# A two-layer encoder trunk on one core: latents scaled on ScalarE, key and value units inside gates, a mask column for the last heads' sums, output projection by half sums

## The chip, the core and the metric

The kernel runs on one core of a Trainium2 chip. The metric is the device time of one execution in microseconds. TensorE (PE, with its weight loads PEld), VectorE (DVE), ScalarE (ACT), GpSimd (POOL) and SyncE (SP, which issues most DMAs) each work through a queue of their own in order and meet at semaphores.

## The reference, cut to what matters

512 tokens of width 1024 pass two layers. Each layer is, in fp32:

```python
h = rms_norm(x, attn_norm_g[l])
proj = h @ w_in[l]
c_q, c_kv, k_rope, gq, gk, gv, pool_in, gate_logits = split_columns(proj, IN_SIZES)
o_mla = mla_branch(c_q, c_kv, k_rope, ...)   # q = rms_norm(c_q) @ w_uq, k and v = rms_norm(c_kv) @ w_ukv
o_gqa = gqa_branch(gq, gk, gv, ...)
o_pool = pool_branch(pool_in, ...)
merged = (gates[:, :, 0] * (o_mla @ w_branch_mla[l])
          + gates[:, :, 1] * (o_gqa @ w_branch_gqa[l])
          + gates[:, :, 2] * (o_pool @ w_branch_pool[l]))
x = x + merged @ w_out[l]
hf = rms_norm(x, ffn_norm_g[l])
u = depthwise_conv(hf @ ffn_w_up[l], ffn_conv_w[l], ffn_conv_b[l])
x = x + (silu(u_gate) * u_val) @ ffn_w_down[l]
```

The latents are c_q (256 columns) and c_kv (128); each is divided by its own root mean square before it meets its weights. Both attentions have eight heads.

## The kernel before

**Numbers in two parts.** Every matmul operand is kept as a large part (hi) and the rest (lo), and a product is three matmuls (mm3, line 378): hi with hi, hi with lo, lo with hi. Activations lie as features by tokens, 512 tokens in the free dimension, in the tiles HH and HL.

**The weights' stream.** All weights lie in HBM as one stream of pieces of up to 512 columns, in the order of use (_widths and _stream, lines 83 to 100; _pack_weights, line 1609). SP loads slots of up to 1024 columns into three buffers (raw, w_dma). w_split (line 326) makes the parts of a piece: ACT copies hi (tile wh), POOL or VectorE subtracts lo (tile wl). wnext (line 363) keeps three pieces ahead.

**An order written by a planner.** The instructions are issued by hand, in an order that a small clock in the program decides (class Clock, line 126): it books an estimated cost on each engine, chains of steps are put in when their estimated time has come, and a question like ck.has(key) asks whether a result should be there. The result is a fixed order on every engine; on the chip semaphores make each instruction wait for what it really needs.

**A layer.**
- tok_major (line 579) computes the latents, tokens by columns, for four blocks of 128 tokens, into four PSUM banks.
- norm_begin and norm_finish (lines 466 and 474) make the RMS norm's factor: VectorE transposes and reduces the sum of squares (tile prt), a matmul of 16 columns adds it over partitions (ps_S<-prt,C), POOL takes the power, VectorE spreads the result (rt by token, rbc by column). norm_finish is tried after each step of the pool matmuls that follow the latents, and carried out once the clock says that prt is there, or by force at one step.
- latents (line 640): ACT empties the four banks (lat_evac) and sums squares, POOL takes the power (ssc), lat_norm scales the four blocks in tile mx on VectorE, eight instructions. lat_turn (line 701) transposes each block on VectorE, writes it to DRAM, reads it back in twelve DMAs as features by tokens, and splits it on ACT (cth) and VectorE (ctl).
- The pool branch's matmuls (line 692), the queries of the second attention (tok_major into gqb, line 747) with their squares, sums and rotations (gq_square, gq_rope), then its keys and values, with the pool's product between (pool_product, line 789). The rotations free the queries' banks.
- gates (line 871) yields the three branches' matmuls in units: a gate tile (eight units of three matmuls), a branch tile (four), and between them the units of the first attention's queries, keys and values (make_q, make_n, make_v; keys and values are 256 columns wide and share two PSUM banks, acc, with the gates). _order (line 66) lists them from EXTRA; a generator of units (Filler, line 103) is spent beside the attention's matmuls to keep TensorE busy.
- attention (line 1131): a plan of times places each head's steps. o_out (line 1306) puts a pair of heads' results and sums into order; the row of the sums that is no result is set to 0 by POOL, then it is added.
- The output projection (line 1438): eight output tiles, one after the other, each over eight merged tiles (kc), which the last branch delivers one by one: product, sum (XM), hi on ACT (mgh), lo on VectorE (mgl).
- The feed-forward part, which is the longest, and then the next layer.

Of the kernel before, what the change touches and what calls it, by code (L numbers as in the profile page):

```python
# [18 lines left out]
P = 128  # L19
# [11 lines left out]
WIDE = 528  # L31
NWIDE = 5
RAW = 3
EXTRA = (("q", 2, (2, 5)), ("n", 2, (6, 7)), ("v", 1, (2, 5)))

SOONER = {1: 3 * KC, 0: 6 * KC}
LAG = {2: 1, 1: 4, 0: 8}
# [2 lines left out]
PRE_B = 8  # L40
LA = 3
END = object()
RSQRT_BITS = 1597463007.0
SLACK = 35
PLAN = {"gqa": (-4.2, -1.0, -0.2, 0.0, 0.65, 2.411, 4.57, 32.003),
        "mla": (-6.2, -2.9, -1.0, 0.1, 0.64, 1.678, 1.82, 35.5)}

D_ROW, D_OUT, D_IN, D_LAT = 3.4, 3.2, 4.0, 6.0
D_FREE = 0.8
REST = 0.4  # L50
W_BIAS = 2.54
C_BIAS = 0.2
# [11 lines left out]


def _order(br):


    r, lag = [], LAG[br]
    for m in range(KC + lag):  # L70
        r += [(k, pos.index(m)) for k, b, pos in EXTRA if b == br and m in pos]
        if m < KC:
            r.append(("g", m))
        if m >= lag:
            r.append(("b", m - lag))
    return r
# [6 lines left out]
def _widths():  # L83

    r = [384] * KC + [T] * 8 + [T] * KC + [288] * 4 + [T] + [288] * 4
    for br in (2, 1, 0):
        for k, _ in _order(br):
            r += WIDTHS[k]
    return r + [T] * (2 * KC) + [T] * (4 * FC) + [T] * (2 * FC)


# [34 lines left out]
class Clock:  # L126
# [37 lines left out]
    def done(self, *key):  # L164
        self.ready[key] = self.fin + self.SEM
# [90 lines left out]
def trunk(ctx: ExitStack, tc: tile.TileContext, x, w, prm, gb, cst, out):  # L256
# [134 lines left out]
    ident = C[:, C_ID:C_ID + P]  # L391
    mhalf = cp.tile([P, 1], F32, tag="mhalf", name="mhalf")
    eps = cp.tile([P, 1], F32, tag="eps", name="eps")


    MQ, MK = [[cp.tile([P, 4, 4, 96], F32, tag=f"{n}{g}", name=f"{n}{g}") for g in range(2)] for n in ("MQ", "MK")]
# [76 lines left out]

    def norm_finish(gen, out, force=False):

        if gen not in parts or not (force or ck.has(("prt", gen))):
            return
        need(("prt", gen))
        s2 = ps("S")
        mm(s2[:, :16], C[:, C_GRP:C_GRP + P], parts.pop(gen), True, True)  # L480
        a, a4 = small("fac", [P, 16]), small("fac4", [P, 16])
        rt, rbc = out["rt"], out["rbc"] = small("rt", [P, 4]), slot("rbc")

        def mean():
            V.tensor_scalar(a, s2[:, :16], 1.0 / D, EPS, ALU.mult, ALU.add)
            free("S")

        def tokens():
            V.tensor_tensor(a4, a, C[:, C_SEL:C_SEL + 16], ALU.mult)
            V.tensor_reduce(rt, a4.rearrange("p (b g) -> p b g", g=4), AX.X, ALU.add)  # L490
            done("rt", gen)

        def rows():
            V.transpose(rbc[:, :T].rearrange("p (j r) -> p j r", r=32), bc(a.unsqueeze(2), [P, 16, 32]))
            done("rbc", gen)

        chain(mean, lambda: G.tensor_tensor(a, a, bc(mhalf, [P, 16]), ALU.pow), tokens, rows, after=0.3)
# [43 lines left out]
    def layer(l, sq, xsrc):  # L541
# [89 lines left out]
            for c0, n in ((0, 256), (1, 128)):  # L631
                V.tensor_scalar(ssc[:, :, c0:c0 + 1], ssc[:, :, c0:c0 + 1], 1.0 / n, EPS, ALU.mult, ALU.add)

        def lat_norm():
            for b in range(4):
                V.tensor_scalar(mx[b][:, 0:256], mx[b][:, 0:256], ssc[:, b, 0:1], None, ALU.mult)
                V.tensor_scalar(mx[b][:, 256:384], mx[b][:, 256:384], ssc[:, b, 1:2], None, ALU.mult)
            done("lat", l)

        def latents():  # L640
            chain(*[([("rt", G1)], lambda b=b: lat_evac(b)) for b in range(4)], lat_mean,
                  *rsqrt_steps(ssc.rearrange("p a b -> p (a b)"), 8, ("ssc", l)), lat_norm)

        latents()

# [46 lines left out]
        for g in range(4):  # L692
            acc = ps(ptags[g])
            for n, _ in enumerate(feat_major(acc, G1)):
                norm_finish(G1, nrm, g == 1 and n == 6)
            chain(*pool_steps(g, acc, ptags[g]))


# [2 lines left out]
        def lat_turn():  # L701
            d = dp.tile([4, P, 384], F32, tag=f"dl{l}", name=f"dl{l}")
            trs, tos = [], []

            def turn_block(b):
                trs.append(slot("tr"))
                V.transpose(trs[b][:, :384], mx[b][:, :384])

            def put(b):
                SY.dma_start(d[b], trs[b][:, :384])  # L710
                ck.fin = ck.now + (D_OUT if b == 3 else 0.1)

            def get(j):
                to = slot("tf")
                src = d.rearrange("b (i f) (c t) -> c f (b i) t", i=4, t=32)
                for c in range(4):
                    SY.dma_start(to[32 * c:32 * c + 32, :T].rearrange("f (g t) -> f g t", t=32), src[4 * j + c])
                chain(*split(lat[j][0][:, :T], lat[j][1][:, :T], to[:, :T], col(PRM_CQ + j)),
                      lambda: done("latT", l, j), after=D_LAT)
                ck.fin = ck.now + 1.5  # L720

            steps = []
            for b in range(4):
                steps += [lambda b=b: turn_block(b), lambda b=b: put(b)]
            chain(*steps, *[lambda j=j: get(j) for j in (2, 0, 1)], after=0.1)

        chain(([("lat", l)], lat_turn))


        qtags = ("AV", "AV", "mi", "ST")  # L730
# [19 lines left out]
        def gq_square(b):  # L750
            j = slot("gqs")
            A.activation(j[:, :T], gqb[b], AF.Square, scale=rtok(b))

            def sums():
                V.tensor_reduce(ssr[:, 8 * b:8 * b + 8], j[:, :T].rearrange("p (h f) -> p h f", f=64),
                                AX.X, ALU.add)
                done("gqs", l, b)

            chain(sums, after=ck.fin - ck.now + 0.1)

        def gq_rope(b):
            q, o = (t.rearrange("p (h f) -> p h f", f=64) for t in (gqb[b], gqo[b][:, :T]))
            cs = bc(tabs[0][:, None, 64 * b:64 * b + 64], [P, 8, 64])
            sn = bc(tabs[0][:, None, 256 + 64 * b:320 + 64 * b], [P, 8, 64])
            parts, add = rope_steps(o, q, cs, sn, [P, 8, 64], 32, V, G)
            parts()
            free(qtags[b])
            chain(add, lambda: done("gqr", l, b), after=ck.fin - ck.now)

        def gq_mean():  # L770
# [100 lines left out]
        def gates(br, okey, odst, mode):  # L871
# [44 lines left out]
                    merged[m] = (mh, ml)  # L916
                    chain(product, add, *split(mh[:, :T], ml[:, :T], XM[:, m, :]), fin)

            extra, tick, gap = None, 0, 2
            for k, m in _order(br):  # L920
                if k in mla_make:
                    extra, tick, gap = mla_make[k](m), 0, 2 if k == "q" else 4
                    continue
                work = branch(m) if k == "b" else gate(m)
                more = True
                while more:
                    if extra and tick % gap == 0:
                        if next(extra, END) is END:
                            extra = None
                        yield  # L930
                    tick += 1
                    more = next(work, END) is not END
                    yield
# [197 lines left out]
        def attention(kind, fill, okey, odst):  # L1131
# [174 lines left out]
            def o_out(h):  # L1306
# [16 lines left out]

                def add():

                    for j in (0, 64):
                        G.memset(sums[j:j + 1, :T], 0.0)
                    (V if h == 7 else G).tensor_tensor(raw[:, :T], raw[:, :T], sums[:, :T], ALU.add)

                steps = [copies]  # L1330
                if h % 2 == 1:
# [103 lines left out]

        sq = slot("sq")
        tags = ("acc", "ST", "AV", "mi", "S")
        for m in range(KC):
            tag = tags[m % 3]
            acc = ps(tag)  # L1440
            for kc in range(KC):
                if kc % 4 == 0:
                    wh, wl = wnext()
                need(("mrg", l, kc))
                ws = slice((kc % 4) * P, (kc % 4) * P + P)
                mm3(acc, wh[:, ws], wl[:, ws], merged[kc][0][:, :T], merged[kc][1][:, :T], kc == 0, kc == KC - 1)

            def resid(m=m, acc=acc, tag=tag):
                V.scalar_tensor_tensor(XM[:, m, :], acc, 0.5, XM[:, m, :], ALU.mult, ALU.add)
                free(tag)  # L1450

            chain(resid, *norm_steps(G2, m, col(PRM_FG + m), sq))
# [105 lines left out]
    A.activation(warm, warm, AF.Exp)  # L1558
    V.memset(mhalf, -0.5)
    V.memset(eps, EPS)  # L1560
    G.memset(f(unit), 0.0)
    G.memset(f(unit[:, 0:1]), 1.0)
    idle = ps("mi")
# [45 lines left out]
def _pack_weights(i):  # L1609
    res = []  # L1610
    for l in range(L):
# [13 lines left out]
        uq, ukv = i["mla_w_uq"][l], i["mla_w_ukv"][l].reshape(P, 8, P)  # L1625

        wb = (i["w_branch_mla"][l], i["w_branch_gqa"][l], i["w_branch_pool"][l])
        for br in (2, 1, 0):
            for k, m in _order(br):
                c = slice(m * P, m * P + P)  # L1630
                if k == "g":
                    res += _cut(_blocks(gate[:, br * D:(br + 1) * D][:, c], KC))
                elif k == "b":
                    res += _cut(_blocks(wb[br][:, c], 4))
                elif k == "q":
                    res += [uq[kc * P:kc * P + P, m * 384:m * 384 + 384] for kc in range(2)]
                else:
                    c = slice(0, 64) if k == "n" else slice(64, P)
                    res.append(ukv[:, 4 * m:4 * m + 4, c].reshape(P, 256))
        for m in range(KC):  # L1640
            res += _cut(_blocks(i["w_out"][l][:, m * P:m * P + P], KC))
        up = i["ffn_w_up"][l]
        for c in range(FC):
            for o in (0, D_FF):
# [85 lines left out]
```

## Time and profile before

| what | value |
|---|---|
| median of three runs | 1575.72 us (1575.36 to 1576.02) |
| the profiled execution's own time | 1576.64 us |
| its span, first to last instruction | 1574.2 us |
| TensorE busy | 1564.2 us, 99% |
| POOL, VectorE, ACT busy | 1021.7, 955.3, 787.4 us |
| granted TensorE clock | 1.00 |
| mean DMA rate | 104 GB/s |

The span is one execution, and the time around it (2.4 us) belongs to start and end. In a row of the timeline stand the start, the duration, the engine, the line of the program (a helper's, so that most rows are told apart by their tiles: what is written, an arrow, what is read), the shape, the count, and in brackets the idle time before it with what ended it. A row with a count merges neighbours of one kind, with the time from the first one's start to the last one's end. In the table of waits stand the time in all, the number of times and the longest.

### The profile page before, as it was taken

The page shows a single profiled execution, that of the slowest core. Times are in us where ns is not written, and L with a number is a line of the kernel's source. Part 1 is how long each engine was busy: PE and PEld are TensorE (multiplying, and loading weights), DVE is VectorE, ACT ScalarE, POOL GpSimd, SP SyncE. Part 2 cuts the span into 40 slices and gives each one's busy share as a digit, 9 for nine tenths or more (in the row PEclk, how much of TensorE's full clock was granted, in tenths as well). Part 3 has the DMA queues.
Part 4 walks back from the last instruction along what each step waited for, and adds up shares of the span by engine and source line. Part 5 has one row for each costly group of instructions (what it writes and reads, how often), then busy time and mean ns, then how long its engine had stood idle before and what let it go on. Part 6 is the DMA issues. An engine that isn't in the chain of part 4 may idle for free.

```text
span 1574.2 us, 20365 instructions
## 1 busy us (share of the span) xinstructions
PE 1564.2 (99%) x7098; PEld 1308.7 (83%) x7098; DVE 955.3 (61%) x1360; ACT 787.4 (50%) x1426; POOL 1021.7 (65%) x890
## 2 busy tenths in 40 slices
PE   9999999999999999999999999999999999999999
PEld 8888888888888888888898888888888888888888
DVE  6877967866267767720047788678652777777000
ACT  5357866763444444432244677676534444444221
POOL 3874987854667666654578649868547766666542
PEclk9999999999999999999999999999999999999999
DMA  5432234314333332333335322343252223233331
GB/s 200 124 113 76 76 95 138 114 56 139 113 95 94 94 105 86 105 107 110 117 103 136 104 75 75 115 136 96 70 158 93 90 95 98 94 96 105 108 128 47
DMA packets 85926, 164.43 MB, mean 104 GB/s; under 512 B 25024, under 2 KB 47040, under 8 KB 85824
## 3 DMA queue, kind: packets, MB, share of 16 engines
q1 hardware_dynamic: 80928, 162.93, 33.6%
q8 instruction: 56, 0.92, 0.3%
q10 hardware_dynamic: 4896, 0.21, 0.2%
q14 instruction: 46, 0.38, 0.1%
HBM read 149.41 MB, written 13.63 MB: 104 GB/s over the span
## 4 chain that ended last, share of the span: by engine, by line
PE 94%; DVE 3%; DMA 1%; ACT 1%; issue 0%; SPq 0%; POOL 0%; ACTq 0%
PE ps_acc L371 42%; PE ps_AV L371 23%; PE ps_ST L371 22%; PE ps_S L371 4%; PE ps_mi L371 4%; DVE XM L224 1%; DVE mgl L224 1%; ACT mgh L217 1%; DMA XM<-x 1%; DVE gt L228 0%; DMA raw<-w 0%; DVE sq L224 0%; ACT oph L217 0%; DVE ph L240 0%; DVE pl L224 0%
## 5 line engine op out<-in xcount | busy, mean ns | idle before, releaser
L224 POOL TENSOR_TENSOR wl<-raw,wh 128x512 fp32r<-128x512 f32 (+2 forms) x503 | 674.8, 1354 | 410.6 <-ACT wh L217 371.5
L217 ACT ACTIVATE wh<-raw 128x512 fp32r<-128x512 f32 (+1 forms) x521 | 308.5, 607 | 126.6 <-PE ps_ST L371 43.6
L228 DVE SCALAR_TENSOR_TENSOR a<-u,prm,a 128x511 f32<-128x511 f32 x176 | 244.2, 1389 | 89.8 <-ACT a L217 83.0
L371 PE MATMUL ps_acc<-HH,wh 128*128 128x512 f32 x592 | 231.6, 391 | 0.5 <-DVE gt L224 0.5
L371 PE MATMUL ps_acc<-HH,wl 128*128 128x512 f32 x592 | 231.1, 390 | 0.0
L371 PE MATMUL ps_acc<-HL,wh 128*128 128x512 f32 x592 | 231.0, 390 | 0.0
L371 PEld LDWEIGHTS ps_acc<-HH,wl 128*128 128x128 f32 x592 | 111.1, 188 | 23.8
L371 PEld LDWEIGHTS ps_acc<-HH,wh 128*128 128x128 f32 x592 | 111.4, 188 | 23.2 <-issue 0.9
L371 PEld LDWEIGHTS ps_acc<-HL,wh 128*128 128x128 f32 x592 | 111.3, 188 | 23.0
L371 PE MATMUL ps_AV<-HH,wh 128*128 128x512 f32 x288 | 112.3, 390 | 0.0
L371 PE MATMUL ps_AV<-HH,wl 128*128 128x512 f32 x288 | 112.1, 389 | 0.0
L371 PE MATMUL ps_AV<-HL,wh 128*128 128x512 f32 x288 | 112.1, 389 | 0.0
L224 POOL TENSOR_TENSOR al<-a,ah 128x512 fp32r<-128x512 f32 x44 | 57.8, 1315 | 83.4 <-ACT ah L217 80.9
L232 DVE TENSOR_REDUCE nm<-ps_S 128x1 fp32r<-128x512 f32 x128 | 87.5, 684 | 38.1 <-PE ps_S L371 36.2
L371 PE MATMUL ps_ST<-HH,wh 128*128 128x512 f32 x240 | 93.6, 390 | 0.0
L371 PE MATMUL ps_ST<-HL,wh 128*128 128x512 f32 x240 | 93.4, 389 | 0.0
L371 PE MATMUL ps_ST<-HH,wl 128*128 128x512 f32 x240 | 93.4, 389 | 0.0
L217 ACT ACTIVATE ah<-a 128x512 fp32r<-128x512 f32 x44 | 27.8, 632 | 128.1 <-DVE a L224 128.1
L217 ACT ACTIVATE a<-u,prm 128x512 f32<-128x512 f32 x88 | 71.0, 809 | 25.9 <-DVE u L224 25.3
L217 ACT ACTIVATE a<-a 128x512 f32<-128x512 f32 x44 | 27.8, 632 | 107.6 <-DVE a L228 107.5
L217 ACT ACTIVATE HH<-XM,prm 128x512 fp32r<-128x512 f32 x32 | 23.1, 722 | 103.7 <-DVE XM L224 53.9
L217 ACT ACTIVATE ps_ST<-ps_ST 128x512 f32<-128x512 f32 x86 | 50.0, 581 | 41.1 <-PE ps_ST L371 39.4
(376 smaller groups left out, 3729.3 us busy)
## 6 DMA issues: line engine op xcount, KB each, us to landing
raw<-w SPq DMA_DIRECT2D x228, 512.0 KB, 3.5
raw<-w SPq DMA_DIRECT2D x13, 384.0 KB, 3.1
XM<-x SPq DMA_DIRECT2D x16, 256.0 KB, 3.4
dtq<-tr SPq DMA_DIRECT2D x16, 192.0 KB, 1.9
dtk<-tr SPq DMA_DIRECT2D x16, 192.0 KB, 2.0
tf<-dtq SPq DMA_DIRECT2D x48, 64.0 KB, 2.0
tf<-dtk SPq DMA_DIRECT2D x48, 64.0 KB, 2.2
raw<-w SPq DMA_DIRECT2D x6, 448.0 KB, 3.4
```

The lines of the kernel that those rows point to most:

```text
L217: return self.eng.activation(out, in_, func, **k)
L224: return self.eng.tensor_tensor(out, *a)
L228: return self.eng.scalar_tensor_tensor(out, *a)
L232: return self.eng.tensor_reduce(out, in_, *a, **k)
L371: PE.matmul(o, lhsT=lhsT, rhs=rhs, start=start, stop=stop)
```

## The change

Six edits:

1. norm_finish is not tried until the clock's time for prt plus D_SUM (2.0) has passed, and the forced step is n == 7 instead of n == 6 (the steps run from 0 to 6).
2. lat_norm scales one block by two ACT instructions, and each block is turned as soon as it is scaled.
3. gq_square's reduction waits, in the clock, for the rotation of the next block.
4. The units of keys and values stand inside gates at fixed steps (2 and 6, or 3) rather than at every fourth step of anything; values come one and two gates earlier than before; in the stream of weights the piece of such a unit comes after the first half of the next gate's.
5. The last pair's sums are added by one VectorE instruction that multiplies by a mask column (0 in partitions 0 and 64, 1 elsewhere), in place of two POOL fills and an addition.
6. The output projection goes by half sums: the first halves of tiles 0 and 1, then the second halves of both, then the other tiles as before; the weights lie in that order.

```diff
-EXTRA = (("q", 2, (2, 5)), ("n", 2, (6, 7)), ("v", 1, (2, 5)))
+EXTRA = (("q", 2, (2, 5)), ("n", 2, (6, 7)), ("v", 1, (1, 3)))
...
+OUT_ORDER = [(0, 0), (1, 0), (0, 1), (1, 1)] + [(m, h) for m in range(2, KC) for h in range(2)]
...
-D_FREE = 0.8
+D_FREE, D_SUM = 0.8, 2.0
...
     for br in (2, 1, 0):
+        late = []
         for k, _ in _order(br):
-            r += WIDTHS[k]
+            if k in "nv":
+                late = WIDTHS[k]
+            else:
+                r += WIDTHS[k][:1] + late + WIDTHS[k][1:]
+                late = []
...
-        if gen not in parts or not (force or ck.has(("prt", gen))):
+        if gen not in parts or not (force or ck.ready.get(("prt", gen), 1e9) + D_SUM <= ck.now):
             return
...
-        def lat_norm():
-            for b in range(4):
-                V.tensor_scalar(mx[b][:, 0:256], mx[b][:, 0:256], ssc[:, b, 0:1], None, ALU.mult)
-                V.tensor_scalar(mx[b][:, 256:384], mx[b][:, 256:384], ssc[:, b, 1:2], None, ALU.mult)
-            done("lat", l)
+        def lat_norm(b):
+            A.activation(mx[b][:, 0:256], mx[b][:, 0:256], AF.Copy, scale=ssc[:, b, 0:1])
+            A.activation(mx[b][:, 256:384], mx[b][:, 256:384], AF.Copy, scale=ssc[:, b, 1:2])
+            done("lat", l, b)
...
-                norm_finish(G1, nrm, g == 1 and n == 6)
+                norm_finish(G1, nrm, g == 1 and n == 7)
...
-                steps += [lambda b=b: turn_block(b), lambda b=b: put(b)]
+                steps += [([("lat", l, b)], lambda b=b: turn_block(b)), lambda b=b: put(b)]
...
-            chain(sums, after=ck.fin - ck.now + 0.1)
+            chain(([("rop", l, min(b + 1, 3))], sums), after=ck.fin - ck.now + 0.1)
...
                 work = branch(m) if k == "b" else gate(m)
-                more = True
+                more, first = True, tick
                 while more:
-                    if extra and tick % gap == 0:
+                    n = tick - first
+                    if extra and (tick % 2 == 0 if when == "q" else k == "g" and n in ((2, 6) if when == "n" else (3,))):
...
+                    if h == 7:
+                        V.scalar_tensor_tensor(raw[:, :T], sums[:, :T], mask, raw[:, :T], ALU.mult, ALU.add)
+                        return
                     for j in (0, 64):
                         G.memset(sums[j:j + 1, :T], 0.0)
-                    (V if h == 7 else G).tensor_tensor(raw[:, :T], raw[:, :T], sums[:, :T], ALU.add)
+                    G.tensor_tensor(raw[:, :T], raw[:, :T], sums[:, :T], ALU.add)
...
-        for m in range(KC):
+        accs = {}
+        for m, part in OUT_ORDER:
             tag = tags[m % 3]
-            acc = ps(tag)
-            for kc in range(KC):
-                if kc % 4 == 0:
-                    wh, wl = wnext()
+            acc = accs[m] = accs.pop(m, None) or ps(tag)
+            wh, wl = wnext()
+            for kc in range(4 * part, 4 * part + 4):
                 need(("mrg", l, kc))
                 ws = slice((kc % 4) * P, (kc % 4) * P + P)
                 mm3(acc, wh[:, ws], wl[:, ws], merged[kc][0][:, :T], merged[kc][1][:, :T], kc == 0, kc == KC - 1)
+            if part == 0:
+                continue
...
-        for m in range(KC):
-            res += _cut(_blocks(i["w_out"][l][:, m * P:m * P + P], KC))
+        for m, part in OUT_ORDER:
+            res.append(_cut(_blocks(i["w_out"][l][:, m * P:m * P + P], KC))[part])
```

More of the change, by code (lines that the diff above doesn't have):

```diff
@@ L393, in trunk @@
     eps = cp.tile([P, 1], F32, tag="eps", name="eps")
+    mask = cp.tile([P, 1], F32, tag="mask", name="mask")
     MQ, MK = [[cp.tile([P, 4, 4, 96], F32, tag=f"{n}{g}", name=f"{n}{g}") for g in range(2)] for n in ("MQ", "MK")]
@@ L632, in lat_mean @@
                 V.tensor_scalar(ssc[:, :, c0:c0 + 1], ssc[:, :, c0:c0 + 1], 1.0 / n, EPS, ALU.mult, ALU.add)
-        def lat_norm():
-            for b in range(4):
-                V.tensor_scalar(mx[b][:, 0:256], mx[b][:, 0:256], ssc[:, b, 0:1], None, ALU.mult)
-                V.tensor_scalar(mx[b][:, 256:384], mx[b][:, 256:384], ssc[:, b, 1:2], None, ALU.mult)
-            done("lat", l)
+        def lat_norm(b):
+            A.activation(mx[b][:, 0:256], mx[b][:, 0:256], AF.Copy, scale=ssc[:, b, 0:1])
+            A.activation(mx[b][:, 256:384], mx[b][:, 256:384], AF.Copy, scale=ssc[:, b, 1:2])
+            done("lat", l, b)
         def latents():
             chain(*[([("rt", G1)], lambda b=b: lat_evac(b)) for b in range(4)], lat_mean,
-                  *rsqrt_steps(ssc.rearrange("p a b -> p (a b)"), 8, ("ssc", l)), lat_norm)
+                  *rsqrt_steps(ssc.rearrange("p a b -> p (a b)"), 8, ("ssc", l)),
+                  *[lambda b=b: lat_norm(b) for b in range(4)])
         latents()
@@ L723, in lat_turn @@
             for b in range(4):
-                steps += [lambda b=b: turn_block(b), lambda b=b: put(b)]
+                steps += [([("lat", l, b)], lambda b=b: turn_block(b)), lambda b=b: put(b)]
             chain(*steps, *[lambda j=j: get(j) for j in (2, 0, 1)], after=0.1)
-        chain(([("lat", l)], lat_turn))
+        chain(([("lat", l, 0)], lat_turn))
         qtags = ("AV", "AV", "mi", "ST")
@@ L767, in gq_rope @@
             free(qtags[b])
+            done("rop", l, b)
             chain(add, lambda: done("gqr", l, b), after=ck.fin - ck.now)
@@ L917, in branch @@
                     chain(product, add, *split(mh[:, :T], ml[:, :T], XM[:, m, :]), fin)
-            extra, tick, gap = None, 0, 2
+            extra, tick, when = None, 0, None
             for k, m in _order(br):
                 if k in mla_make:
-                    extra, tick, gap = mla_make[k](m), 0, 2 if k == "q" else 4
+                    extra, tick, when = mla_make[k](m), 0, k
                     continue
                 work = branch(m) if k == "b" else gate(m)
-                more = True
+                more, first = True, tick
                 while more:
-                    if extra and tick % gap == 0:
+                    n = tick - first
+                    if extra and (tick % 2 == 0 if when == "q" else k == "g" and n in ((2, 6) if when == "n" else (3,))):
                         if next(extra, END) is END:
@@ L1560, in trunk @@
     V.memset(eps, EPS)
+    V.memset(mask, 1.0)
+    for j in (0, 64):
+        V.memset(mask[j:j + 1], 0.0)
     G.memset(f(unit), 0.0)
@@ L1627, in _pack_weights @@
         wb = (i["w_branch_mla"][l], i["w_branch_gqa"][l], i["w_branch_pool"][l])
+        late = []
         for br in (2, 1, 0):
@@ L1631, in _pack_weights @@
                 if k == "g":
-                    res += _cut(_blocks(gate[:, br * D:(br + 1) * D][:, c], KC))
+                    a, b = _cut(_blocks(gate[:, br * D:(br + 1) * D][:, c], KC))
+                    res += [a] + late + [b]
+                    late = []
                 elif k == "b":
@@ L1638, in _pack_weights @@
                     c = slice(0, 64) if k == "n" else slice(64, P)
-                    res.append(ukv[:, 4 * m:4 * m + 4, c].reshape(P, 256))
-        for m in range(KC):
-            res += _cut(_blocks(i["w_out"][l][:, m * P:m * P + P], KC))
+                    late = [ukv[:, 4 * m:4 * m + 4, c].reshape(P, 256)]
+        for m, part in OUT_ORDER:
+            res.append(_cut(_blocks(i["w_out"][l][:, m * P:m * P + P], KC))[part])
         up = i["ffn_w_up"][l]
```

## The prediction

> **What bounds the kernel now.** I read the page first, then the longest waits of TensorE.
>
> ```profile
> span 1574.2 us, 20365 instructions
> PE 1564.2 (99%) x7098; PEld 1308.7 (83%) x7098; DVE 955.3 (61%) x1360; ACT 787.4 (50%) x1426; POOL 1021.7 (65%) x890
> ...
> PE ps_S L371 <- DVE prt L232: 1.9, 1, 1.9
> ...
> PE ps_acc L371 <- ACT wh L217: 1.0, 1, 1.0
> PE ps_ST L371 <- ACT oph L217: 0.8, 1, 0.8
> PE ps_acc L371 <- POOL wl L224: 0.7, 1, 0.7
> PE ps_acc L371 <- DVE gt L224: 0.5, 2, 0.3
> PE ps_acc L371 <- DVE mgl L224: 0.5, 2, 0.2
> ```
>
> TensorE is the bound: 1564.2 of 1574.2 us. The changed program holds the same matmuls in the same shapes, in another order, so it can only give back waits. The waits understate themselves, because a matmul counts as busy for some 0.39 us though the next one can start earlier. I therefore count from start to start. The chain of waits gives the pitch:
>
> ```profile
> 398.87 5.44 PE ps_AV L371 x24
> ```
>
> That is 5.44 / 24 = 0.227 us for 512 columns. How much the early waits cost is read by setting layer 0 beside layer 1, from the first pool matmul (22.64 and 807.29) to the same point before attention, a table of two stretches:
>
> ```profile
> 22.64:87.61 64.97, 60.49 (x304) 51.16 (x304) 53.82 (x93) 27.19 (x62) 51.75 (x46) 1.00 0.41 113
> 807.29:866.85 59.56, 59.56 (x304) 51.25 (x304) 44.53 (x82) 26.93 (x62) 47.21 (x39) 1.00 0.47 125
> ```
>
> The columns are length, then busy time and count of PE, PEld, DVE, ACT and POOL, and the granted clock. The same 304 matmuls at the same clock take 64.97 us in layer 0 and 59.56 in layer 1: 5.41 us of waiting in one stretch. It lies in three places of the TensorE timeline:
>
> ```profile
> 28.84 0.40 PE L371 MATMUL ps_S<-prt,C 128*128 128x16 f32 x2 [1.92 <-DVE prt L232]
> ...
> 70.02 0.29 PE L371 MATMUL ps_ST<-wl,HH 128*128 128x288 f32 x1
> 70.15 0.30 PE L371 MATMUL ps_ST<-wh,HL 128*128 128x288 f32 x1
> 71.48 0.40 PE L371 MATMUL ps_acc<-wh,HH 128*128 128x288 f32 x1 [1.03 <-ACT wh L217]
> 72.59 0.40 PE L371 MATMUL ps_acc<-wl,HH 128*128 128x288 f32 x1 [0.71 <-POOL wl L224]
> ...
> 80.35 0.47 PE L371 MATMUL ps_ST<-mxh,wh 128*128 128x512 f32 x1 [0.81 <-ACT oph L217]
> ```
>
> The idle time in brackets begins at the end of a matmul that is drawn 0.39 long and has a pitch of 0.23, so each wait is 0.16 longer: 1.92 + 0.16 = 2.08. The 288-column pitch is 0.13 (70.02 to 70.15): 1.03 + 0.17 = 1.20, and 0.71 + 0.27 = 0.98. The last is 0.81 + 0.16 = 0.97. These make 5.23 of the 5.41; slow restarts are the rest.
>
> **The change part by part.**
>
> *The norm's sum matmul (D_SUM, n == 7).* The order of the changed program puts nine pool matmuls ahead of the 16-column matmul in layer 0; in layer 1 its place stays. Nine by 0.227 fill 2.04 of the 2.08 us. Against that, the loader's third small-part subtraction on POOL (L341, wl) now stands ahead of the norm's power instead of behind it, and starts when the two before it end, at 25.3, beside VectorE's sums of squares:
>
> ```profile
> 21.18 0.68 DVE L224 TENSOR_TENSOR sq<-sq,sqt 128x512 f32<-128x512 f32 x1
> ...
> 22.39 4.93 DVE L224 TENSOR_TENSOR sq<-sq,sqt 128x512 f32<-128x512 f32 x4
> ...
> 22.18 3.14 POOL L224 TENSOR_TENSOR wl<-raw,wh 128x512 fp32r<-128x512 f32 x2 [21.09 <-ACT wh L217]
> ```
>
> Alone a sum takes 0.68; the four took 4.93 where 2.8 was due, and POOL's two subtractions ran beside the first two. So each shared sum cost about 1.0 more. A third POOL subtraction should catch the third sum: 1.0 later. I take 2.04 - 1.0 = 1.0 us gained; bounds 2.0 (nothing caught) and 0 (two caught). The norm's factors come as much later as the sums; their first users empty the latents' and pools' banks, which TensorE meets again some 10 us after that. Before the feed-forward part the same matmul moves nine later in both layers: six banks of 24 matmuls (5.44 each) lie between it and the first bank that is met again, so 0. The Trainium skill, SBUF — State Buffer, section Who interferes with whom, says that a VectorE instruction with two SBUF inputs contends with a GpSimd instruction that reads SBUF; the rows agree (1.0 us a shared sum), and by that rule the third sum is caught and the gain is the 1.0.
>
> *Latents on ACT, block by block.* In layer 0 the wait at 71.48 hangs on a chain that begins with the latents' scaling:
>
> ```profile
> 43.75 2.09 POOL L224 TENSOR_TENSOR ssc<-ssc,mhalf 128x8 f32<-128x8 f32 x1
> ...
> 47.13 6.67 DVE L236 TENSOR_SCALAR mx<-mx,ssc 128x256 f32<-128x256 f32 x8
> ...
> 54.34 1.94 DVE L248 STREAM_TRANSPOSE tr<-mx 128x384 f32<-128x384 f32 x4
> ...
> 56.76 0.46 SPq L710 DMA_DIRECT2D dl<-tr  x1
> 60.64 4.04 SPq L717 DMA_DIRECT2D tf<-dl  x8
> 64.78 0.43 SPq L322 DMA_DIRECT2D raw<-w  x1
> 65.25 2.02 SPq L717 DMA_DIRECT2D tf<-dl  x4
> ...
> 70.38 0.72 ACT L217 ACTIVATE cth<-tf,prm 128x512 fp32r<-128x512 f32 x1 [1.89 <-DMA tf<-dl]
> 71.00 1.09 ACT L217 ACTIVATE wh<-raw 128x288 fp32r<-128x288 f32 x3
> ```
>
> Eight scalings hold VectorE for 6.67 us, the transposes come after all of them, twelve reads queue on SP, and the last latent split keeps ACT waiting until 70.38 with the weight splits behind it. On ACT I price a scaling by the squares of the same shapes:
>
> ```profile
> 34.57 0.42 ACT L217 ACTIVATE junk<-mx 128x256 f32<-128x256 f32 x1
> ...
> 34.98 0.29 ACT L217 ACTIVATE junk<-mx 128x128 f32<-128x128 f32 x1
> ```
>
> 0.42 + 0.29 = 0.71 a block, 2.8 us for four. The norm factors come at 45.8, up to 1.0 later by the step above; ACT then has a pool split and a weight split ahead (0.6 each), so it starts near 48. With the weight split that now stands between the third and fourth block it ends near 51.5, and a weight subtraction (0.7) and the last transpose (0.5) end near 52.7, not at 56.3. The write and its landing take 3.9 (56.76 to 60.64), twelve reads at 0.5 and one weight load among them (0.43, as before, but after the first four) 6.5: the last read is issued near 63.2, not 67.3, and lands 3.1 later, as before (67.27 to 70.38), near 66.3. The next 288-column weights are needed at about 69 (70.28 less the 1.0 above), and one of the two splits that stood behind the last latent now stands ahead of it. Both waits go: 1.20 + 0.98 + 0.1 for a restart = 2.3 us. What is late next is POOL's weight subtraction, still about 2.5 us early. The transposes now wait for ACT; behind them on VectorE stand the third pool's edges, which wait for POOL's window sums anyway: 0. Bounds: 0 if the transfers slip back, 2.3 if they don't; the 4 us gained against 1.3 lost in the wait decide for 2.3. The Trainium skill, ScalarE: Activation LUTs, section Rules for kernel authors, speaks against this step: multiplications belong on VectorE, and an ACTIVATE costs about 0.3 us plus 0.83 ns an element. By it a block would cost an estimated 0.9 us, where the squares show 0.71, and four 3.7; the sum would still be 2.3, as the split has the time.
>
> *Sums behind the next block's rotation.* The wait at 80.35 is put down to ACT, but the fourth block's rotation on VectorE ends 0.15 us before it, and that frees the bank:
>
> ```profile
> 75.82 1.27 DVE L232 TENSOR_REDUCE ssr<-gqs 128x8 f32<-128x512 f32 x2
> ...
> 79.52 0.68 DVE L224 TENSOR_TENSOR gqr<-ps_ST,tabg 128x512 f32<-128x512 f32 x1
> ```
>
> Two of three reductions (0.6 each) now stand behind the rotations: 1.2 us sooner, and the rotations start sooner too since ACT is not held. TensorE comes 3.3 us sooner, so this has the smallest margin, about 1 us. I take 1.0, in layer 0 alone; layer 1's stretch shows no idle time. Bounds 0 and 1.2. The reductions are late instead, by about 1.8 us, for the norm that attention needs; 2 us remain there.
>
> *Key and value units inside gates.* Before, a 256-column unit could leave a gate's bank too little time:
>
> ```profile
> 213.33 0.28 PE L371 MATMUL ps_acc<-wh,cpl 128*128 128x256 f32 x1
> 213.88 0.47 PE L371 MATMUL ps_acc<-HH,wh 128*128 128x512 f32 x1 [0.27 <-DVE gt L224]
> ```
>
> 0.55 less a pitch of 0.12 (0.13 by 256/288) is 0.43, and 0.1 at restart, in each layer. By the orders, the bank's last user and next one lay 1.17 and 0.94 us of matmuls apart; in the changed order the nearest pair lies 2.04 apart, and pairs that lie 1.4 to 1.6 apart are named in no wait. I take 0.5 a layer, 1.0 in all; bounds +1.2 and, if a unit meets a late operand in its new place, -1.
>
> *Mask column.* Two POOL fills and a wait leave the last pair's sums, before TensorE needs them: 0, hidden behind gates that need no heads. If that cover went, the chain is only shorter. Three fills at the start lie beside the first loads: 0.
>
> *Output projection by halves.* The first output tile needs the last merged tile too early:
>
> ```profile
> 392.01 0.41 PE L371 MATMUL ps_acc<-mgh,wh 128*128 128x512 f32 x1
> 392.65 0.50 PE L371 MATMUL ps_acc<-mgl,wh 128*128 128x512 f32 x1 [0.23 <-DVE mgl L224]
> ```
>
> 0.64 - 0.23 = 0.41, and 0.1 at restart. Twelve matmuls (2.72 us) now stand before that use: the wait goes, 0.5 a layer, 1.0 in all. The wait for the first tile's bank (0.3 a layer) is at the same place as before: 0, bounds 0 and 0.6 for both. The first residual comes 2.7 us later, with seven tiles still to run.
>
> **Sum:** 1.0 + 2.3 + 1.0 + 1.0 + 1.0 = 6.3 us. The profiled execution took 1576.64 us, 2.4 around its span; it goes to 1570.3. The median shown is 0.9 below the profiled run: 1575.72 - 6.3 = **1569.4 us**.
>
> **The rivals.**
> *The latents' transfers slip back.* If ACT reaches the scalings late, or SP's weight load waits for POOL ahead of eight reads, the waits at 71.48 and 72.59 stay, and TensorE meets the rotations as before: 2.3 and 1.0 are lost, 6.3 - 3.3 = 3.0, 1572.7 us. For it: the scaling queue now passes through an engine with weight splits. Against: 4 us of room.
>
> *The norm's sum is caught twice*, by the contention above: the first term is 0 and the rest stands, 1570.4 us. It lies within the forecast's range.
>
> *The change does nothing where it aims* (waits only move to the next engine): within 0.2%, 1574 us.
>
> *Slower: the first head's keys.* Their last unit moves eight matmuls later, and the keys' scaling, transposes, two transfers and the split follow it in order.
>
> ```profile
> 233.75 0.61 ACT L217 ACTIVATE kh<-tf 96x512 fp32r<-96x512 f32 x1
> ...
> 236.72 0.39 PE L371 MATMUL ps_S<-kh,qa 96*128 96x512 f32 x1
> ```
>
> Ready at 234.36 and used at 236.72: 2.4 us in hand. Beyond that every microsecond costs one in each layer. It decides from (6.3 + 3.2) / 2 + 2.4 = 7.2 us late; at 8 us late the price is 11.2 and the time 1580.6. Against: the unit moves by some 2 us, and the transfers start long after the scaling.
>
> **How the numbers follow.** Forecast, with the twice-caught sum: 0.74. Transfers slip: 0.12, a little more than half of it inside 0.2% (3.15 us, about what a measurement of this kernel tells from no change). Nothing: 0.07. Slower: 0.07. Faster by over 0.2%: 0.74 + 0.05 = 0.79; within: 0.07 + 0.07 = 0.14; slower: 0.07. The range's low end takes the upper bounds, 1.0 more for the norm, 0.2 each for rotations and units, 0.6 for the banks: 1569.4 - 2.0 = 1567.4. The high end includes the slipped transfers and 0.3 more: 1573.0.
>
> **What would show it.** Layer 0's stretch of 304 matmuls near 60.7 us, with a wait of about 1.0 for prt; no TensorE wait for wh, wl or oph near 70 to 80; no wait for gt after a 256-column unit, none for mgl; latents on ACT ending near 50 and the last latent split before 67. I am wrong if a wait for kh, vm or MK over 1 us appears in both layers, or if the wait for wh near 70 stays.

## The result, and the profile after

The changed kernel takes 1592.48 us (median of 4 runs, 1591.53 to 1593.82) against 1575.87 for the kernel before in the same session: a ratio of 1.0101, with an interval of 1.0089 to 1.0113. The prediction was 1569.4 us. The profiled execution took 1592.20 us around a span of 1590.2.

The page of the changed kernel says first that the waits didn't grow. Here are its first lines, and its waits of TensorE (in total, times, longest):

```profile
span 1590.2 us, 20339 instructions
...
PE 1583.5 (100%) x7098; PEld 1309.7 (82%) x7098; DVE 944.1 (59%) x1352; ACT 794.1 (50%) x1438; POOL 1010.1 (64%) x881
```

```profile
PE ps_S L379 <- DVE prt L240: 1.1, 1, 1.1
PE ps_mi L1584 <- DVE mask L260: 1.1, 1, 1.1
PE ps_acc L379 <- DVE XM L236: 0.9, 2, 0.5
```

The second line is the start of the kernel and took 1.1 us before too, there for eps. The waits for wh, wl, oph, gt and mgl that the prediction quoted are gone. Counted from start to start, against the usual pitch of each shape, all waits of TensorE together fell from about 14 us to about 7.5 (a sum over the two traces, good to some 0.5 us). But TensorE is busy for 1583.5 us where it was 1564.2, with the same 7098 matmuls: the matmuls themselves became slower. Which ones shows in the groups kept apart by shape (busy time, mean ns of one). Before:

```profile
L371 PE MATMUL ps_acc<-HH,wh 128*128 128x512 f32 x592 | 231.6, 391 | 0.5 <-DVE gt L224 0.5
...
L371 PE MATMUL ps_acc<-ah,wh 128*128 128x512 f32 x132 | 51.4, 389 | 0.0
...
L371 PE MATMUL ps_AV<-vt,unit 128*128 128x512 f32 x32 | 12.5, 392 | 0.0
```

After:

```profile
L379 PE MATMUL ps_acc<-HH,wh 128*128 128x512 f32 x592 | 234.4, 396 | 0.9 <-DVE XM L236 0.9
...
L379 PE MATMUL ps_acc<-ah,wh 128*128 128x512 f32 x132 | 51.4, 389 | 0.0
...
L379 PE MATMUL ps_AV<-vt,unit 128*128 128x512 f32 x32 | 12.7, 396 | 0.0
```

Of the large groups those with HH or HL are longer, by 5 ns of the modelled length; those with ah, of the same shape and with weights from the same buffers, are not. A small group with vt and unit is longer as well. The feed-forward part, which the change doesn't touch, shows the pitch. Two stretches of it, the first with HH and HL, the second with ah and al; before:

```profile
500.00:550.00 50.00, 50.00 (x222) 41.39 (x222) 36.37 (x33) 21.96 (x36) 33.13 (x24) 1.00 0.31 95
...
720.00:770.00 50.00, 50.00 (x222) 41.39 (x221) 4.33 (x6) 14.68 (x25) 30.25 (x25) 1.00 0.38 120
```

After:

```profile
500.00:550.00 50.00, 50.00 (x216) 40.30 (x215) 33.78 (x32) 22.36 (x36) 30.78 (x23) 1.00 0.31 96
...
720.00:770.00 50.00, 50.00 (x223) 41.39 (x222) 5.77 (x8) 16.19 (x28) 25.99 (x21) 1.00 0.35 111
```

216 instead of 222 matmuls in 50 us, at a granted clock of 1.00 and with no idle time, in the first; no difference in the second. The chain of waits has the exact figure, 24 matmuls of one bank in the same part of the kernel, before and after:

```profile
507.91 5.44 PE ps_AV L371 x24
```

```profile
508.76 5.60 PE ps_AV L379 x24
```

5.60 / 24 = 233.3 ns against 226.7, 2.9% more. The matmuls with HH and HL moving number 3 x (592 + 288 + 240) = 3360, or 140 such groups: 140 x 0.16 = 22.4 us. Less the 6.5 to 7 that the waits gave back, that is near the 16.0 us by which the span grew.

**What could slow these matmuls alone.** Their instructions are the same; their addresses are not. In the compiled program a pool's tiles stand one behind the other in the order of declaration, each padded to a multiple of 32 bytes a partition (mhalf and eps hold 4 bytes each and start at 55,232 and 55,264), and the pools follow each other. The mask is a new tile:

```python
eps = cp.tile([P, 1], F32, tag="eps", name="eps")
mask = cp.tile([P, 1], F32, tag="mask", name="mask")
```

XM, HH and HL are declared ahead of it. HH starts at byte 17,536 of a partition in both kernels. Everything declared behind the mask moved by 32 bytes, the weights and the working tiles (ah, al, oh, mgh ...) among them: the first wh from 93,824 to 93,856. Modulo 256, HH and wh both started at 128 before; after it is 128 and 160. ah and its weights moved together. The pair vt and unit fits as well, as far as 32 matmuls tell: unit is declared ahead of the mask, vt behind it. The theory was therefore PLACE, the relative position of a matmul's two operands; the rival was LOAD, that TensorE without its pauses or beside the busier ACT is slower by itself.

### The profile page after: what moved, and what is told of

The parts are those of the page before. It is cut to its first block, busy times and chain, and to the rows that moved or that the text cites. A ratio compares the mean times of both kernels' runs of the same rounds, so it can differ in the third digit from the quotient of the medians.

```text
span 1590.2 us, 20339 instructions
## 1 busy us (share of the span) xinstructions
PE 1583.5 (100%) x7098; PEld 1309.7 (82%) x7098; DVE 944.1 (59%) x1352; ACT 794.1 (50%) x1438; POOL 1010.1 (64%) x881
## 4 chain that ended last, share of the span: by engine, by line
PE 95%; DVE 3%; ACT 1%; DMA 0%; issue 0%; SPq 0%; DVEq 0%; ACTq 0%
PE ps_acc L379 42%; PE ps_AV L379 23%; PE ps_ST L379 22%; PE ps_S L379 4%; PE ps_mi L379 4%; DVE XM L232 1%; DVE mgl L232 1%; DVE sq L232 0%; ACT mgh L225 0%; DVE gt L236 0%; DMA XM<-x 0%; DVE ka L248 0%; ACT wh L225 0%; ACT HH L225 0%; DVE wl L232 0%
## 5 line engine op out<-in xcount | busy, mean ns | idle before, releaser
L232 POOL TENSOR_TENSOR wl<-raw,wh 128x512 fp32r<-128x512 f32 (+2 forms) x502 | 665.3, 1336 | 429.9 <-ACT wh L225 394.0
L225 ACT ACTIVATE wh<-raw 128x512 fp32r<-128x512 f32 (+2 forms) x521 | 309.0, 607 | 135.1 <-PE ps_ST L379 43.5
L236 DVE SCALAR_TENSOR_TENSOR a<-u,prm,a 128x511 f32<-128x511 f32 x176 | 236.1, 1344 | 83.0 <-ACT a L225 80.0
L379 PE MATMUL ps_acc<-HH,wl 128*128 128x512 f32 x592 | 234.3, 396 | 0.0
```

The costliest lines, as they stand in the source:

```text
L225: return self.eng.activation(out, in_, func, **k)
L232: return self.eng.tensor_tensor(out, *a)
L236: return self.eng.scalar_tensor_tensor(out, *a)
L379: PE.matmul(o, lhsT=lhsT, rhs=rhs, start=start, stop=stop)
```

## The experiments

The kernel before took 1576.72 us beside e1 to e4, 1576.68 beside e5 to e8 and 1576.69 beside e9 to e12. e7 and e8 are one run each, e5 two; their cores show a granted clock of 0.999 or 1.000.

**e1: the mask without a tile of its own.**

```diff
-    eps = cp.tile([P, 1], F32, tag="eps", name="eps")
-    mask = cp.tile([P, 1], F32, tag="mask", name="mask")
+    eps2 = cp.tile([P, 2], F32, tag="eps2", name="eps2")
+    eps, mask = eps2[:, 0:1], eps2[:, 1:2]
```

> The changed kernel with its mask kept in a second column of the tile that holds eps, so that no tile is added and every tile stands where it stood in the kernel before. Theory PLACE: the added mask tile, 32 bytes with its padding, pushed the weights and all working tiles by 32 bytes while HH and HL stayed; a matmul whose two operands start in different halves of a 64-byte line takes 233 instead of 227 ns, 3,300 of them some 21 us. It expects the pitch of the HH matmuls back at 227 ns and about 1570 us (1592.5 less 22). Rival LOAD: TensorE without its pauses, or beside the busier ACT, runs slower by itself, whatever the addresses: pitch 233 ns, 1592 us.

1569.28 us (1569.16 to 1569.52), ratio 0.9954 (0.9939 to 0.9968). The page's first lines and one group of the chain:

```profile
span 1567.3 us, 20339 instructions
...
PE 1560.7 (100%) x7098; PEld 1307.4 (83%) x7098; DVE 949.3 (61%) x1352; ACT 790.5 (50%) x1438; POOL 1022.6 (65%) x881
```

```profile
507.93 5.44 PE ps_acc L379 x24
```

All of the change's instructions are in it, and the 22.9 us of span between it and the changed kernel hang on that one tile. LOAD has fallen.

**e2: the kernel before, with nothing but an unused tile of 32 bytes.**

```diff
     eps = cp.tile([P, 1], F32, tag="eps", name="eps")
+    pad = cp.tile([P, 8], F32, tag="pad", name="pad")
...
+    V.memset(pad, 1.0)
```

> The kernel before with one unused tile of 32 bytes a partition declared behind eps (one fill at the start), nothing else. PLACE: HH matmuls 233 ns, about 1576 + 22 = 1598 us, though no instruction of the change is in it. LOAD: 227 ns, 1576 us.

1597.50 us, ratio 1.0136 (1.0119 to 1.0153): the slowdown without the change.

```profile
507.32 5.60 PE ps_ST L371 x24
```

**e3: 64 bytes** (pad of 16 columns in the same place).

> The kernel before with an unused tile of 64 bytes at the same place. PLACE with a 64-byte line: both operands start in the same half again, 227 ns, 1576 us. If any shift of the weights against HH costs (distance, not halves): 233 ns, 1598 us. LOAD: 1576 us.

1598.74 us, ratio 1.0140 (1.0125 to 1.0156). My picture of 64-byte lines fell: 64 bytes apart is as slow as 32.

```profile
505.56 5.60 PE ps_acc L371 x24
```

**e4: 32 bytes ahead of everything** (the pad declared ahead of XM).

> The kernel before with an unused tile of 32 bytes ahead of all others, so that HH, HL, the weights and everything else move by 32 together. PLACE (the two operands' halves must agree): 227 ns, 1576 us. Rival ABSOLUTE (a tile that starts off a multiple of 64 is slow by itself): every matmul slow, 7,000 by 6 ns, about 1616 us; or, if only the weights' start counts, 1598 us or more.

1576.62 us, ratio 1.0000 (0.9991 to 1.0010). None of the kernel's tiles keeps its address, and the time doesn't change: it is the two operands' distance that counts, not where they start.

```profile
507.99 5.44 PE ps_AV L371 x24
```

**e5 and e6: 128 and 256 bytes apart** (pad of 32 columns; and C declared ahead of XM with a pad of 16, which sets HH and the weights 256 bytes apart modulo 512).

> The kernel before with an unused tile of 128 bytes behind eps. The idea of 64-byte lines has fallen with the 64-byte tile (1598.7 us, 233 ns). What all fast matmuls have in common is that the start addresses of their two operands agree modulo 512 bytes, the width of a weight block of 128 columns. Theory PERIOD 512: 128 bytes apart is slow too, 233 ns, about 1598 us. PERIOD 128: 227 ns, 1576 us.

> The kernel before with the tile of constants C declared ahead of XM and an unused tile of 64 bytes behind eps: HH and HL then lie 256 bytes from the weights modulo 512. PERIOD 512: 233 ns, about 1598 us. PERIOD 256 (or 128): 227 ns, 1576 us.

e5: 1595.26 us, ratio 1.0115 (1.0086 to 1.0144). e6: 1576.65, ratio 1.0002 (0.9991 to 1.0013). The groups of e5, then of e6:

```profile
506.36 5.57 PE ps_ST L371 x24
```

```profile
507.87 5.44 PE ps_AV L371 x24
```

So 128 apart is slow and 256 apart is as fast as 0. Both periods that I had set against each other in e5, 512 and 128, are wrong; a period of 256 bytes fits, though distances such as 96, 160 or 192 were not tried.

**e7: only wl moved, by 32 bytes** (a pool of its own for wl, an unused 32-byte tile between the pools).

```diff
+    padp = ctx.enter_context(tc.tile_pool(name="padp", bufs=1))
+    hllp = ctx.enter_context(tc.tile_pool(name="hllp", bufs=LA + 3))
...
-        lo = hlp.tile([P, T], F32R, tag="wl", name=f"wl{j}")
+        lo = hllp.tile([P, T], F32R, tag="wl", name=f"wl{j}")
```

> The kernel before with the low halves wl of the weights in a pool of their own, 32 bytes further (an unused tile between the pools moves them, and the working tiles behind them too). HH, HL and wh still agree, wl does not. The order is HH by wh, HL by wh, HH by wl. Theory OWN (a matmul's moving operand against its own weights): HH by wl takes 233 ns, the other two 227. Theory NEXT (the moving operand against the weights that are loaded beside it, for the matmul behind it): HL by wh takes 233 ns, HH by wl 227. Either way two of three matmuls on the working tiles are slow too: about 1576 + 7 + 7 = 1590 us.

1605.62 us, not 1590. The chain has full 5.60 groups for HH, and 66 matmuls with ah take 15.40 where they take 14.96 otherwise:

```profile
497.49 5.60 PE ps_AV L373 x24
...
728.48 15.40 PE ps_acc L373 x66
```

Neither OWN nor NEXT holds. With HH, HL and wh in step and wl alone out of step, the pitches are not 227, 227, 233 in any order; their means are 233 behind HH by wh, 237 behind HL by wh, 228 behind HH by wl, and the three together come to 698 ns, nearly the 700 of a group that is out of step altogether (680 in step). The ah groups settle one thing: in e2 ah kept its distance from both wh and wl and stayed fast, here it has moved against wh alone and is slow, so the distance that counts is that from the weights. Which of the reads meet is open.

**e8: 16 bytes** (HH in column 4 of a wider tile, HL 32 bytes off, mhalf ahead of XM).

> The kernel before with HH 16 bytes and HL 32 bytes from the weights modulo 512 (HH starts in column 4 of a tile that is 32 bytes wider, and mhalf stands ahead of XM). If any distance costs, HH's and HL's matmuls all take 233 ns, 1598 us. If only steps of 32 bytes count, HH's stay at 227 ns and HL's alone take 233: 1120 of them by 6 ns, 1583 us.

1591.52 us, neither 1598 nor 1583, and groups between fast and slow:

```profile
506.06 5.55 PE ps_ST L371 x24
```

24 of them cost 0.11 us more than in step, where the full loss is 0.16. From start to start the mean pitch is 232 ns behind HH by wh and 233 behind HH by wl, but 228 behind HL by wh, the reverse of what was expected if only steps of 32 bytes cost. As one operand out of step slows the whole group (e7), and HL is 32 bytes off here, this run doesn't tell whether HH's 16 bytes would cost by themselves; that stays open.

**e9, e10, e11: the change's other parts, undone one by one from e1.** e9 puts the latents' scaling back on VectorE (lat_norm and its chain as before), e10 the units and the output projection (OUT_ORDER back to whole tiles, EXTRA, _widths, _stream and the loop over units as before), e11 the norm's sum:

```diff
-        if gen not in parts or not (force or ck.ready.get(("prt", gen), 1e9) + D_SUM <= ck.now):
+        if gen not in parts or not (force or ck.has(("prt", gen))):
...
-                norm_finish(G1, nrm, g == 1 and n == 7)
+                norm_finish(G1, nrm, g == 1 and n == 6)
```

> The changed kernel with the mask beside eps (1569.3 us) and the latents' scaling back on VectorE, all eight instructions ahead of the first transpose. The prediction's second term says that the waits for wh and wl near 70 come back, 2.3 us, and perhaps the one for the rotations (1.0 more): 1571.6 to 1572.6 us. Rival: the waits stay away because the rest of the change has moved the weights, 1569.3 us.

> The same base with the key and value units back between gates and the output projection back to whole tiles. The prediction's terms say that the waits for gt after a 256-column unit (0.5 a layer) and for mgl (0.5 a layer) come back: 1571.3 us. Rival: those waits only change places, 1569.3 us.

> The same base with the norm's sum matmul back at its old place (no D_SUM, n == 6). The prediction's first term says 1.0 us more: the wait for prt is 2.1 instead of 1.5 us, 1569.9 to 1570.3 us. Rival: nothing, 1569.3 us.

e9: 1571.98 us, ratio 0.9966 (0.9953 to 0.9978). e10: 1572.20, ratio 0.9970 (0.9959 to 0.9982). e11: 1571.66, ratio 0.9962 (0.9950 to 0.9975). Each is 2 to 3 us above e1, but the intervals of the ratios overlap e1's. Every run of e9 and e10 is longer than every run of e1; those of e11 (1569.11 to 1572.99) are not. What a part is worth is therefore read from the waits. Waits of e9 (of the two in the first row, that of 0.7 is at 71.28, the other near 100), then of e10:

```profile
PE ps_acc L379 <- POOL wl L232: 1.1, 2, 0.7
...
PE ps_ST L379 <- DVE gqr L232: 0.3, 1, 0.3
```

```profile
PE ps_acc L374 <- DVE gt L227: 0.5, 2, 0.3
PE ps_acc L374 <- DVE mgl L227: 0.5, 2, 0.2
```

e9's time lies in the range that was expected, but not by the waits that were: the wait for wl near 71 is back, that for wh is not, and the rotations cost some 0.4 instead of 1.0. Counted from start to start, e9 waits some 1.5 us more than e1 between 60 and 80 us and 1.1 more near 100, and 0.85 less for prt; that the sum comes out as expected is chance. In e10 both waits are back in both layers, 0.5 each time, as expected; the rest of its excess is a longer wait for prt (1.86 against 1.46, start to start) and, in its profile, a stretch at half speed like the one that e11 shows.

In e11 the wait for prt grows by 1.06 (2.36 against 1.30 idle), as the first term said, and something more follows: from the seventh matmul behind it on, they are drawn 0.63 long and start 0.43 apart.

```profile
28.97 0.40 PE L379 MATMUL ps_S<-prt,C 128*128 128x16 f32 x2 [2.36 <-DVE prt L240]
...
31.12 0.63 PE L379 MATMUL ps_AV<-HL,wh 128*128 128x512 f32 x1
31.55 0.63 PE L379 MATMUL ps_AV<-HH,wl 128*128 128x512 f32 x1
```

The windows show why, by the granted clock (third figure from the end), in e11:

```profile
32.00:34.00 2.00, 2.00 (x6) 1.61 (x5) 1.37 (x3) 0.00 (x0) 1.81 (x2) 0.50 0.00 0
```

and in e1:

```profile
32.00:34.00 2.00, 2.00 (x11) 1.64 (x10) 0.47 (x1) 0.00 (x0) 2.00 (x2) 1.00 0.00 0
```

**e12: a faster version.** e1 with the output tiles begun in other banks, and with the force on the norm's sum set later.

```diff
-            tag = tags[m % 3]
+            tag = tags[(m + 1) % 3]
...
-                norm_finish(G1, nrm, g == 1 and n == 7)
+                norm_finish(G1, nrm, g == 2 and n == 2)
```

> A try at a faster version: the same base, the first norm's sum matmul nine matmuls later still (g == 2, n == 2), and the output projection's tiles begin in another pair of banks. If the waits for prt (1.5 us) and for the first output tile's bank (0.4 a layer) go and nothing follows, 1569.3 less 2.2 = 1567.1 us; if the later factors hold the banks of the latents and pools, 1569 us or more.

1568.11 us (1567.85 to 1568.73), ratio 0.9944 (0.9931 to 0.9958), the lowest median of all, against 1569.28 for e1, and 1.0 short of what was hoped for. The waits for the first output tile's bank are gone, 0.4 a layer. The later force did nothing: the sum stood at the same matmul as in e1, since D_SUM had let it through before, and a wait for prt is left, 0.4 shorter than in e1 for a reason that was not followed up:

```profile
PE ps_S L379 <- DVE prt L240: 0.9, 1, 0.9
```

## Why the prediction was wrong

The step that failed is the mask column. The prediction priced the mask by its instructions, "three fills at the start lie beside the first loads: 0", and never asked what its tile does to the layout. With it fell the sentence on which the sum rests, that the changed program, with the same matmuls in the same shapes, "can only give back waits", and the pitch of 0.227 us that was carried over as a constant. e1 and e2 together show what this term is worth: 22.9 us of span with the change's instructions (1590.2 less 1567.3) and 21.1 without them (1595.3 less 1574.2). The slower rival, the late keys, wasn't it either: no wait for kh, vm or MK appears.

The other terms can be read in e1, where the tile's effect is taken out. The sum was 6.3 us; its span is 6.9 below that of the kernel before. That its time, 1569.28, lies 0.1 from the forecast of 1569.4 is luck: the kernel before took 1576.72 beside it, 1.0 more than the 1575.72 from which the forecast was counted, and the saving there is 7.4. Layer 0's stretch of 304 matmuls takes 60.99 us where 60.7 was forecast, and these waits of TensorE are left (the last two lie in the first 8 us, ahead of the stretch):

```profile
22.28:83.27 60.99, 59.69 (x304) 51.25 (x304) 49.01 (x88) 30.29 (x71) 52.84 (x45) 1.00 0.43 121
```

```profile
PE ps_S L379 <- DVE prt L240: 1.3, 1, 1.3
...
PE ps_acc L379 <- DVE wl L232: 0.3, 1, 0.3
PE ps_acc L379 <- DVE HL L236: 0.2, 1, 0.2
```

**Norm's sum, 1.0.** Four of VectorE's sums and three of POOL's subtractions, in e1:

```profile
22.47 5.91 DVE L232 TENSOR_TENSOR sq<-sq,sqt 128x512 f32<-128x512 f32 x4
```

```profile
22.27 4.84 POOL L232 TENSOR_TENSOR wl<-raw,wh 128x512 fp32r<-128x512 f32 x3 [21.18 <-ACT wh L225]
```

5.91 against 4.93: the third subtraction cost the third sum the 1.0 us that was expected. The wait that remains is 1.30 + 0.16 = 1.46 against 2.08:

```profile
29.90 0.40 PE L379 MATMUL ps_S<-prt,C 128*128 128x16 f32 x2 [1.30 <-DVE prt L240]
```

It is shorter by 0.6, not 1.0, because TensorE entered the stretch 0.36 us earlier (its first pool matmul starts at 22.28, not 22.64). Undone in e11, the step costs 1.06 us of waiting, as priced. What the prediction missed is that a shorter wait can also keep the clock up (below).

**Latents on ACT, 2.3.** The forecast was a start near 48, the end near 51.5, the last transpose's end near 52.7 and the last latent split before 67. In e1 ACT's scalings stand in these rows:

```profile
47.23 2.18 ACT L225 ACTIVATE mx<-mx,ssc 128x256 f32<-128x256 f32 x6
49.32 0.61 ACT L225 ACTIVATE wh<-raw 128x512 fp32r<-128x512 f32 x1
49.84 0.79 ACT L225 ACTIVATE mx<-mx,ssc 128x256 f32<-128x256 f32 x2
...
65.90 0.72 ACT L225 ACTIVATE cth<-tf,prm 128x512 fp32r<-128x512 f32 x1
```

and the last transpose in this one of VectorE:

```profile
52.42 0.57 DVE L256 STREAM_TRANSPOSE tr<-mx 128x384 f32<-128x384 f32 x1
```

A block takes 0.74 (2.97 for four) where 0.71 was priced; the scalings end at 50.63, the last transpose at 52.99, and the last split starts at 65.90, each within 1 us of the forecast. Both waits are gone, and e9 brings a part of them back.

**Rotations, 1.0; units, 1.0; halves, 1.0.** The waits at 80.35, behind the 256-column units and for mgl are gone in e1; in e10 the last two return in both layers. No run undoes the new order of the rotations by itself, so that this edit removed the wait at 80.35 is argued, not shown; the same holds for the mask's one instruction in place of three, which was priced at 0. The first output tile's bank was expected unchanged at 0.3 a layer, and is; e12 removes it.

What is late next is a wait of 0.3 behind the first layer's first pool product (near 98), which the prediction didn't see; in the changed kernel it stands in both layers, as the wait for XM. Start to start, the five terms come to some 5.9 us in e1 (0.6, 2.3, 1.0, 1.0 and 1.0); the other 1 us of the 6.9 is what smaller restarts and the earlier start of the stretch gave, which are no term of the sum.

## What to carry to other kernels

A new tile, however small, moves every tile declared behind it; compare the start addresses of each matmul's two operands before and after (0 and 256 bytes apart were fast here; 32, 64 and 128 were not), and put a small constant into a spare column of a tile that is there. When a change moves the time the wrong way while the waits shrink, compare the pitch of the same matmuls in a stretch that the change doesn't touch, before looking for a wait. A term costed at nothing needs its storage costed as well as its instructions.

## What the runs showed of the hardware

**The pitch of a matmul depends on its operands' distance.** These are float32r matmuls of 128 rows by 512 columns, three to a product. With the moving operand and the weights 0 or 256 bytes apart modulo 512, a group of three takes 680 ns; with 32, 64 or 128 bytes between them 697 to 700; with 16 and 32 mixed 694. Moving both together changes nothing (e4). Which reads meet in the memory, and why a group of three is slowed whole when one of its four operands is out of step (e7), stays open. Other types were not tried.

**Half speed after a short wait.** In nine of the fourteen profiles, one for each kernel, the wait for prt near 29 us was between 1.86 and 3.12 us, start to start; in seven of them, e11 among them, TensorE then ran at a granted clock of 0.50 for 3.41 us, which is 7 or 8 matmuls at 0.43 instead of 0.23 us, some 1.5 us lost. In the other five, with a wait of 1.73 us or less, e1 and the changed kernel among them, it never did. The profile of before that the prediction read, with a wait of 2.08 us, is one of the two that kept the clock. The Trainium skill, TensorE: Matmul & The Clock Gate, section What's actually happening, says that the clock falls to half after an idle window of about 3.4 us and returns after a busy one, and that the windows run freely, so that the moment varies. The traces agree on the half speed (0.50), its length (3.41 us) and the chance in it (seven of nine); but here waits of 1.86 to 3.12 us, shorter than such a window, were enough.
